# Layer 0's scan and attention as one stage, with the modulation products moved from VectorE to GpSimd and ScalarE

## The chip, the cores and the metric

The kernel runs on one core of a Trainium2 chip. The metric is the device time of one execution in microseconds (us); smaller is better. The core has five engines that run side by side and wait for each other through semaphores: PE (TensorE, matrix products), DVE (VectorE), ACT (ScalarE), POOL (GpSimd) and SP (SyncE, which here only issues transfers). Each engine takes its instructions strictly in the order in which the program has them.

## The reference, cut to what matters

A two-layer network works on 256 context tokens and 1024 latent tokens of width 1024. Layer 0's mixer has two independent halves that read the same projections, and it is these two that the change touches:

```
# half A: differential attention, 4 heads, 2 score maps per head, 128 queries a block in the reference
s = einsum('bhmqd,bhmkd->bhmqk', q, k) * 64**-0.5
p = softmax(s, axis=-1)
w = p[:, :, 0] - lam * p[:, :, 1]
o = einsum('bhqk,bhkd->bhqd', w, v)          # then an RMS norm per head

# half B: RWKV-7, 8 heads, a scan over the tokens, forward and backward
def step(S, inp):
    r_t, w_t, k_t, v_t, kk_t, a_t = inp
    sa = einsum('bhvk,bhk->bhv', S, kk_t)
    S = S * w_t - sa * (kk_t * a_t) + v_t * k_t
    return S, einsum('bhvk,bhk->bhv', S, r_t)
...
o = concatenate([attention, rwkv], axis=-1) @ w_out
```

Beside them stand the modulation vectors of the layer: `silu(c) @ mod_w + mod_b`, for the latent conditioning and for the context conditioning. Four of these vectors (g1, sh2, sc2, g2) are computed while the scan runs. Context queries (256) see only context keys, latent queries (1024) see all 1280.

## The kernel before

Everything is feature-major: a tile has 128 features on its partitions and tokens along its rows. Products that need precision use a split of fp32 into a high and a low part. The program is written as Python generators that yield between small pieces of work; a scheduler then orders each engine's instructions by its own estimate of when they can run, and semaphores are placed for that order. So the order on each engine is fixed before the run.

*Scan.* The 1280 tokens are cut into ten windows of 128 tokens, for both directions at once. A window has two chunks of 64 tokens, and each chunk is one `step`: four small groups of products on PE with an elementwise operation between each two (`rpm` on DVE, `sav` on ACT and DVE, the state `S` on DVE, the output copy `ryt` on ACT). What does not depend on the state is prepared ahead: `front` (scores L568, transposes L580, then `blocks`, a DVE chain that inverts 8 by 8 blocks) and `back` (`values` L609/L610, `inverse` L656, L662, L676, L687, which doubles the inverted blocks up to 64 and ends with the tile `iu`). In the loop `scan`, window sw runs beside `back` of window sw+1 and `front` of window sw+2: preparation stands up to two windows ahead. Before the first window, front 0, back 0 and front 1 run alone. `post` normalizes finished windows and stores them in `rw_o`.

*Modulation.* Every eighth round of the loop, `mods_dot` (L220) does two tiles: one DVE instruction multiplies a 128x1024 tile of transposed weights (`mdw`) with a row of the conditioning and sums it. That is 64 such instructions in this stage.

*Attention.* When the scan is through, `heads` runs over four heads and five pairs of query blocks. A score tile (L967, L968; 128 queries by up to 1280 keys, three PSUM banks) goes through a maximum on DVE (L970) and an exponential on ACT (L971). There are two such PSUM tiles, `at0` and `at1`. `differ` joins the two maps on DVE (L982); `mix` transposes the weights on PE (L999), copies them on ACT (`a_w`, L1001) and multiplies them with the values for 256 queries at once (`po`, L1004). `norm` then handles a whole head of 1280 tokens at a time and writes `at_o`.

PSUM has eight banks. In the scan five are `rw`, two `rz` and one `ry`; in the attention at0 and at1 have three each, and `mm` and `po` one each. After the attention comes the output projection (L87 to L89 with the tile `o`).

## Time and profile before

| what | us |
|---|---|
| median of 3 timed runs | 3969.39 (3968.36 to 3971.47) |
| the profiled execution: its own time | 3967.53 |
| its span, first to last instruction | 3965.7 |
| from the scan's first load (556.2) to the output projection's first product (1406.8) | 850.6 |
| of that, PE busy | 622.0 |
| mean granted clock of PE over the span | 0.935 |

A busy time is the union of an engine's instructions in a stretch, so the rest of the stretch is the time in which that engine stood idle. The granted clock is a share of 2.4 GHz; the engine has two levels, 1.2 and 2.4 GHz, so 0.79 means that part of the stretch ran at 0.5. PE's 622.0 us is the sum over the four stretches that the first group of rows shows.

### The profile page before, as it was taken

How to read it: one execution, taken by the hardware profiler on the slowest of the kernel's cores; microseconds unless marked ns; L12 is line 12 of the kernel's file. 1: busy time of each engine (PE TensorE's matmuls, PEld its weight loads, DVE VectorE, ACT ScalarE, POOL GpSimd, SP SyncE). 2: the span in 40 equal slices, each digit the busy share in tenths (PEclk: the TensorE clock that was granted, in tenths of full speed). 3: DMA queues.
4: the chain of work that ended last, by engine and by line, in shares of the span. 5: the costliest groups of instructions: out<-in, count | busy, mean ns of one | idle time of the engine just before them, and what ended most of it. 6: DMA issues, size and time to landing. Idle time of an engine off the chain costs nothing.

```text
span 3965.7 us, 68983 instructions
## 1 busy us (share of the span) xinstructions
PE 3587.8 (90%) x28912; PEld 2976.9 (75%) x28912; DVE 2048.2 (52%) x3741; ACT 1138.8 (29%) x1926; POOL 1305.6 (33%) x1121
## 2 busy tenths in 40 slices
PE   6999967766778879999999999999998889999998
PEld 4878846665667668888888888778776778888886
DVE  6344435766657647555444436357247663333335
ACT  3333321111255505111111113575543141111112
POOL 2455532322310015233222323217434352333223
PEclk8999977787788989999999999999999889999998
DMA  5244462333262142122222212232442311111111
GB/s 199 79 122 127 118 188 85 111 109 114 81 187 78 51 146 68 59 85 75 71 68 85 75 38 77 67 92 70 121 126 84 109 54 43 46 56 48 43 43 64
DMA packets 288999, 353.14 MB, mean 89 GB/s; under 512 B 91825, under 2 KB 217265, under 8 KB 288561
## 3 DMA queue, kind: packets, MB, share of 16 engines
q1 hardware_dynamic: 288688, 348.74, 28.3%
q8 instruction: 227, 3.72, 0.4%
q14 instruction: 84, 0.68, 0.1%
HBM read 265.03 MB, written 83.62 MB: 88 GB/s over the span
## 4 chain that ended last, share of the span: by engine, by line
PE 58%; DVE 3%; DMA 1%; ACT 1%; issue 1%; POOL 0%; SPq 0%; POOLq 0%; ACTq 0%; DVEq 0%
PE mm L87 10%; PE mm L88 10%; PE mm L89 10%; PE ss L87 4%; PE ss L88 4%; PE ss L89 4%; PE sp L88 4%; PE sp L87 4%; PE sp L89 4%; PE sp L1222 1%; PE ss L1475 1%; PE sp L1406 1%; PE si L1491 1%; PE mm L1232 1%; DMA wraw<-in_wout_dram 0%
## 5 line engine op out<-in xcount | busy, mean ns | idle before, releaser
L88 PE MATMUL mm<-actl,whi 128*128 128x512 f32 (+1 forms) x2432 | 903.3, 372 | 18.6 <-DVE actl L298 10.8
L87 PE MATMUL mm<-acth,whi 128*128 128x512 f32 (+1 forms) x2432 | 899.8, 372 | 19.2 <-ACT acth L95 6.9
L89 PE MATMUL mm<-acth,wlo 128*128 128x512 f32 (+1 forms) x2432 | 892.8, 370 | 0.0
L99 POOL TENSOR_TENSOR wlo<-wraw,whi 128x1024 fp32r<-128x1024 f32 (+2 forms) x243 | 495.7, 2047 | 1072.7 <-ACT whi L95 1065.4
L87 PEld LDWEIGHTS mm<-acth,whi 128*128 128x128 f32 x2432 | 465.1, 191 | 112.9 <-issue 8.1
L88 PEld LDWEIGHTS mm<-actl,whi 128*128 128x128 f32 x2432 | 465.3, 191 | 107.9 <-DVE actl L298 11.9
L89 PEld LDWEIGHTS mm<-acth,wlo 128*128 128x128 f32 x2432 | 465.0, 191 | 81.9 <-issue 4.4
L95 ACT CAST whi<-wraw 128x1024 fp32r<-128x1024 f32 (+2 forms) x243 | 217.1, 906 | 1049.5 <-PE mm L88 386.0
L345 POOL TENSOR_TENSOR relu<-relu 128x256 f32<-128x256 f32 (+1 forms) x163 | 162.2, 995 | 368.8 <-ACT relu L344 368.8
L97 DVE CAST hidh<-relu 128x256 fp32r<-128x256 f32 (+1 forms) x163 | 71.1, 436 | 354.8 <-POOL relu L345 353.6
L88 PE MATMUL sp<-hidl,whi 128*128 128x512 f32 (+1 forms) x648 | 238.5, 368 | 1.5 <-DVE hidl L99 1.5
L344 ACT ACTIVATE relu<-mm 128x256 f32<-128x256 f32 (+1 forms) x163 | 88.9, 545 | 520.8 <-PE mm L89 378.7
L87 PE MATMUL sp<-hidh,whi 128*128 128x512 f32 (+1 forms) x648 | 238.3, 368 | 0.0
L89 PE MATMUL sp<-hidh,wlo 128*128 128x512 f32 (+1 forms) x648 | 238.0, 368 | 0.0
L87 PE MATMUL ss<-hidh,whi 128*128 128x512 f32 (+1 forms) x600 | 222.8, 371 | 0.4 <-DVE hidh L97 0.4
L88 PE MATMUL ss<-hidl,whi 128*128 128x512 f32 (+1 forms) x600 | 222.5, 371 | 0.2 <-DVE hidl L99 0.2
L89 PE MATMUL ss<-hidh,wlo 128*128 128x512 f32 (+1 forms) x600 | 221.8, 370 | 0.0
L369 DVE SCALAR_TENSOR_TENSOR x<-ss,g,x 128x256 f32<-128x256 f32 x180 | 118.9, 661 | 145.2 <-PE ss L89 145.2
L369 DVE SCALAR_TENSOR_TENSOR x<-sp,g,x 128x512 f32<-128x512 f32 (+1 forms) x192 | 126.8, 661 | 105.5 <-PE sp L89 105.4
L220 DVE CUSTOM_DVE_ANT_0 mdj<-mdw,silu_r,t_cols 128x1024 f32<-128x1024 f32 x128 | 172.7, 1349 | 1.2
L369 DVE SCALAR_TENSOR_TENSOR x<-ss,g2b,x 128x512 f32<-128x512 f32 x120 | 90.0, 751 | 142.6 <-PE ss L89 142.6
L369 DVE SCALAR_TENSOR_TENSOR x<-sp,g2b,x 128x512 f32<-128x512 f32 (+1 forms) x132 | 96.7, 733 | 101.9 <-PE sp L89 101.9
(510 smaller groups left out, 6636.0 us busy)
## 6 DMA issues: line engine op xcount, KB each, us to landing
mdw<-in_modt_dram SPq DMA_DIRECT2D x80, 512.0 KB, 3.6
wraw<-in_wa_dram SPq DMA_DIRECT2D x64, 512.0 KB, 3.6
wraw<-in_wb_dram SPq DMA_DIRECT2D x64, 512.0 KB, 3.5
wraw<-in_win_dram SPq DMA_DIRECT2D x51, 512.0 KB, 3.8
x<-in_xT_dram SPq DMA_DIRECT2D x16, 640.0 KB, 10.7
rw_kr<-rw_t SPq DMA_DIRECT2D x16, 640.0 KB, 3.3
rw_bk<-rw_t SPq DMA_DIRECT2D x32, 320.0 KB, 3.9
rkr<-rw_kr SPq DMA_DIRECT2D x20, 512.0 KB, 5.1
```

What stands on the lines that cost most here:

```text
L87: self.nc.tensor.matmul(out, lh, rh, start=start and i == 0, stop=False)
L88: self.nc.tensor.matmul(out, lh, rl, start=False, stop=False)
L89: self.nc.tensor.matmul(out, ll, rh, start=False, stop=stop and i == n - 1)
L95: nc.scalar.copy(out=hi, in_=src)
L97: nc.vector.tensor_copy(out=hi, in_=src)
L99: e.tensor_tensor(out=lo, in0=src, in1=hi.bitcast(F32), op=ALU.subtract)
L220: nc.vector.tensor_tensor_reduce(out=junk, in0=raw, in1=rows[:, j], scale=1.0, scalar=modb[:, 8 * w + t : 8 * w + t + 1], op0=ALU.mult, op ...
L344: nc.scalar.activation(out=r, in_=ps, func=AF.Relu)
L345: nc.gpsimd.tensor_tensor(out=r, in0=r, in1=r, op=ALU.mult)
L369: nc.vector.scalar_tensor_tensor(out=xg, in0=ps, scalar=gate[:, m, j : j + 1], in1=xg, op0=ALU.mult, op1=ALU.add)
L1222: nc.tensor.matmul(pd, k["after" if d == 0 else "before"], rl.rearrange("p h t -> p (h t)"), start=d == 0, stop=d == 1)
L1232: nc.tensor.matmul(o, xd[d][:, hd * 64 : hd * 64 + 64], us[hd // 4, d][:, hd % 4], start=d == 0, stop=d == 1)
```

## The change

- *One stage.* `heads` is no longer run behind the scan but beside it: the loop `scan` takes a list of side tasks and advances the attention every third round and the modulation every fourth. Posts are advanced one at a time in each round (`output`).
- *One step ahead.* `front`, `values` and `inverse` of window sw+1 become one sequence, `prep`, that runs beside window sw. Buffers shrink accordingly (`rkr` 6 to 4, `rs` and `rbt` 10 to 6, `imb` 2 to 1 and others), and `rw` has three PSUM banks instead of five.
- *128 queries.* Attention goes block by block: `queries` loads one block of 128 in eight transfers (40 blocks instead of 20 pairs), there is one score tile `at` in PSUM instead of two, and `mix` multiplies 128 queries at a time. `norm` works in groups of up to 512 tokens.
- *Modulation.* `mods_mul` multiplies on POOL (L245 after the change) and sums on ACT (L246), in place of the single DVE instruction; each weight tile is loaded twice, once for each conditioning, so 64 loads instead of 32.

```
+    def mods_mul(self, pool, tag, bufs, modt, modb, which, names):
...
+            for j in range(2):
+                row = pool.tile([P, 1024], F32, name="silu_r", tag="silu_r", bufs=1)
...
+                for (t0, w), o in zip(which, outs):
+                    for t in range(8):
+                        raw = pool.tile([P, 1024], F32, name="mdw", tag="mdw", bufs=bufs)
+                        nc.sync.dma_start(out=raw, in_=modt[t0 + t])
+                        with self.tc.issue_after(self.last(E.Pool)), self.tc.issue_after(self.last(E.Activation)):
+                            nc.gpsimd.tensor_tensor(out=raw, in0=raw, in1=row, op=ALU.mult)
+                            nc.scalar.activation(out=raw, in_=raw, func=AF.Copy, accum_out=o[:, t, j : j + 1])
+                        yield
...
-        mb = T([P, 2, 2, 4, 64], "imb", 2)
-        kr = [T([P, 2, 4, P], "rkr", 6) for d in range(2)]
+        mb = T([P, 2, 2, 4, 64], "imb", 1)
+        kr = [T([P, 2, 4, P], "rkr", 4) for d in range(2)]
...
-                    s = T([P, 4, P], f"rs{hh}", 10)
+                    s = T([P, 4, P], f"rs{hh}", 6)
...
-                bt[d, c] = T([P, 4, P], "rbt", 10)
+                bt[d, c] = T([P, 4, P], "rbt", 6)
...
+    def prep(self, sw, o):
+        yield from self.front(sw, o)
+        yield from self.values(o)
+        yield from self.inverse(o)
+
+    def output(self):
+
+        while self.posts or self.written < 10:
+            if self.posts:
+                yield from self.posts.pop(0)
+            yield
+
+    def scan(self, pool, asides):
...
         for sw in range(10):
-            turn = [self.window(sw, os[sw])] + [self.back(os[sw + 1])] * (sw < 9) + [self.front(sw + 2, os[sw + 2])] * (sw < 8) + self.posts
-            self.posts = []
-            for q in count():
+            turn = [self.window(sw, os[sw])] + [self.prep(sw + 1, os[sw + 1])] * (sw < 9)
+            while turn:
                 turn = [g for g in turn if next(g, 0) is None]
-                if not turn:
-                    break
-                if q % 8 == 4:
-                    next(aside, None)
+                next(output, None)
+                q += 1
+                for every, steps in asides:
+                    if q % every == 0:
+                        next(steps, None)
+            os[sw].clear()
+        turn = [output] + [steps for _, steps in asides]
+        while turn:
+            turn = [g for g in turn if next(g, 0) is None]
...
+            for qb in range(10):
+                o = self.queries(hd, qb)
+                for m in range(2):
+                    self.scores(o, K, m)
+                    yield
+                    next(ahead, None)
+                    next(ahead, None)
+                    next(norm, None)
+                self.differ(o, qb)
                 yield from ahead
...
+        e = o["e"][m] = self.tile(f"a_e{m}", F32, bufs=3 - 2 * m)
+        ps = n.psum(1536, "at")
...
+            nc.tensor.matmul(ps[:, s], qh, K[m][:, s], start=True, stop=False)
+            nc.tensor.matmul(ps[:, s], ql, K[m][:, s], start=False, stop=True)
...
+        po = n.psum(512, "po")[:, :P]
...
+                for kb in range(k0 - 4, min(k0, nb)):
+                    nc.tensor.matmul(po, v[:, kb], ws[k0 // 4 - 1][:, kb % 4 * P : kb % 4 * P + P], start=kb == 0, stop=kb == nb - 1)
...
-        heads = L("at")
-        n.banks(("rw",), rw=5, rz=2, ry=1)
...
-        n.banks(("mm",), at0=1, at1=1, mm=1, po=1)
-        finish(at.heads(heads.__enter__(), rw.posts))
...
+        n.banks(("rw",), at=1, mm=1, po=1, rw=3)
+        with L("at") as ap, L("post") as rw.out, R("scan") as sp, n.pools(mo=1):
+            (g1, sh2, sc2, g2), mods = n.mods_mul(n.mo, "mm", 2, I["modt0"], k0["mod_b"], [(8 * q, 2 + q) for q in range(4)], ("g1", "sh2", "sc2", "g2"))
+            heads = at.heads(ap)
+            rw.scan(sp, ((3, heads), (4, mods)))
```

The order on the engines changes with it. First PE's row where the scan starts. Before, behind the last products of the projections stand the silu rows (L197) and then at once the scan's first scores (L568) and transposes (L580):

```order
L891 MATMUL sp<-ones,lam_pr 128x1 x2
L197 MATMUL rz<-ident,silu_c 128x128 x16
L568 MATMUL rw<-rkr,rbk 128x128 x8
L580 MATMUL rw<-ident,rbk 128x128 x4
L568 MATMUL rw<-rkr,rbk 128x128 x8
L580 MATMUL rw<-ident,rbk 128x128 x4
```

In the changed program score tiles of the first head (L1000, L1001) stand ahead of and between these same products, which are now L594 and L606:

```order
L1000 MATMUL at<-ak_4845,aq0h 128x256
L1001 MATMUL at<-ak_4845,aq0l 128x256
L1028 MATMUL mm<-ident,a_e_5111 128x128 x2
L1033 MATMUL po<-a_w,av 128x128 x2
L594 MATMUL rw<-rkr,rbk 128x128 x8
L606 MATMUL rw<-ident,rbk 128x128 x4
L1000 MATMUL at<-ak_4848,aq1h 128x512
L1001 MATMUL at<-ak_4848,aq1l 128x512
```

Fifteen score tiles (four of 256 keys, eleven of 1280) now come ahead of the first window's first product. The second place is PE's row in the middle of the scan, between two of the products that double an inverse. Before, pieces of other windows of the scan stand there (scores, a step's first and second product):

```order
L568 MATMUL rw<-rkr,rbk 128x128 x8
L709 MATMUL rw<-S,rkr 64x64 x16
L662 MATMUL rw<-id,iwt 32x32 x64
L580 MATMUL rw<-ident,rbk 128x128 x4
L715 MATMUL rw<-rpm,iu 64x64 x16
```

In the changed program the same product (L662 is now L684) stands between pieces of attention alone, here in window 3:

```order
L678 MATMUL rw<-itt,rs_8158 32x32
L1033 MATMUL po<-a_w,av 128x128 x2
L1000 MATMUL at<-ak_7335,aq0h 128x512
L1001 MATMUL at<-ak_7335,aq0l 128x512
L1000 MATMUL at<-ak_7335,aq0h 128x512
L1001 MATMUL at<-ak_7335,aq0l 128x512
L1000 MATMUL at<-ak_7335,aq0h 128x256
L1001 MATMUL at<-ak_7335,aq0l 128x256
L684 MATMUL rw<-id,iwt 32x32 x64
L1028 MATMUL mm<-ident,a_e_8919 128x128 x4
```

So a score tile and its mixing took the place of other windows' scan work. Counted over the windows 0 to 9, 0, 4, 6, 9, 4, 7, 4, 5, 6 and 2 tiles of 1280 keys stand between the first product of a window and that of the next; six more stand behind the last window. The third place is POOL's row in window 0. Before, the masked copies `imb` follow one another:

```order
L575 TENSOR_TENSOR imb<-rs_4777,t_masks_85 64x256
L575 TENSOR_TENSOR imb<-rs_4780,t_masks_85 64x256
L575 TENSOR_TENSOR imb<-rs_4800,t_masks_85 64x256
L575 TENSOR_TENSOR imb<-rs_4803,t_masks_85 64x256
L575 TENSOR_TENSOR imb<-rs_4823,t_masks_85 64x256
```

In the changed program (L575 is now L601) products of the modulation stand between them:

```order
L601 TENSOR_TENSOR imb<-rs_4839,t_masks_85 64x256
L601 TENSOR_TENSOR imb<-rs_4842,t_masks_85 64x256
L245 TENSOR_TENSOR mdw<-mdw,silu_r 128x1024 x2
L601 TENSOR_TENSOR imb<-rs_4964,t_masks_85 64x256
L601 TENSOR_TENSOR imb<-rs_4967,t_masks_85 64x256
L245 TENSOR_TENSOR mdw<-mdw,silu_r 128x1024
L601 TENSOR_TENSOR imb<-rs_5032,t_masks_85 64x256
L601 TENSOR_TENSOR imb<-rs_5035,t_masks_85 64x256
L245 TENSOR_TENSOR mdw<-mdw,silu_r 128x1024
```

So a masked copy that the inversion waits for can now stand behind a product of 128x1024.

## Rows read from the trace of the kernel before

**Rows 1.** Busy time by engine in five stretches: scan start, windows 0-8, window 9, attention, projection.
```profile
core 0: us, PE busy (x) PEld busy (x) DVE busy (x) ACT busy (x) POOL busy (x), PEclk, DMA share, GB/s
556.20:613.90 57.70, 34.62 (x865) 30.06 (x865) 22.59 (x54) 7.63 (x13) 14.35 (x22) 0.62 0.41 121
613.90:1071.40 457.50, 319.42 (x10015) 286.73 (x10015) 311.69 (x699) 84.43 (x152) 123.20 (x142) 0.79 0.34 106
1071.40:1099.00 27.60, 17.59 (x342) 14.59 (x340) 10.66 (x36) 6.68 (x14) 10.07 (x8) 0.88 0.35 96
1099.00:1406.80 307.80, 250.34 (x1301) 201.06 (x1301) 193.60 (x306) 159.56 (x282) 32.29 (x55) 0.89 0.34 102
```

**Rows 2.** PE groups of the scan: busy, mean ns | idle before, releasers.
```profile
L715 PE MATMUL rw<-rpm,iu 64*64 64x64 f32 x576 | 28.8, 272 | 49.0 <-DVE rpm L712 49.0
L656 PE MATMUL rw<-itt,rs 32*32 32x32 f32 x2560 | 32.7, 204 | 32.5 <-DVE itt L652 19.2 <-issue 13.1
L709 PE MATMUL rw<-S,rkr 64*64 64x64 f32 x576 | 29.4, 271 | 25.2 <-DVE S L729 15.0 <-DVE ipr L631 5.9 <-issue 4.3
```

**Rows 3.** Timeline (start, duration) of window 0's preparation, which runs alone.
```profile
556.17 0.33 SPq L557 DMA_DIRECT2D rkr<-rw_kr  x1
561.47 2.08 PE L568 MATMUL rw<-rkr,rbk 64*128 64x128 f32 x16 [10.60 <-DMA rbk<-rw_bk]
573.64 0.73 POOL L575 TENSOR_TENSOR imb<-rs,t_masks 64x256 f32<-64x256 f32 x1
584.82 0.71 DVE L652 STREAM_TRANSPOSE itt<-id 128x512 f32<-128x512 f32 x1 [1.20 <-POOL id L636]
591.22 0.71 DVE L652 STREAM_TRANSPOSE itt<-id 128x512 f32<-128x512 f32 x1
607.61 0.69 DVE L692 COPY iu<-rw 32x512 f32<-32x512 f32 x1 [2.21 <-ACT iu L694]
```

**Rows 4.** Timeline of PE in the attention: one score tile, transposes, a mix, a norm.
```profile
1123.94 0.50 PE L967 MATMUL at<-ak,aqh 128*128 128x512 f32 x1
...
1125.08 0.28 PE L968 MATMUL at<-ak,aql 128*128 128x256 f32 x1
1342.08 0.60 PE L999 MATMUL mm<-ident,a_e 128*128 128x128 f32 x4
1342.51 1.03 PE L1004 MATMUL po<-a_w,av 128*128 128x256 f32 x4
1346.07 1.16 PE L1031 MATMUL mm<-ident,rsy_at 128*128 128x128 f32 x8
```

**Rows 5.** Groups of DVE and ACT that a score tile goes through.
```profile
L970 DVE TENSOR_REDUCE a_mx<-at 128x1 f32<-128x1280 f32 x64 | 94.6, 1486 | 21.8 <-PE at L968 21.4
L971 ACT ACTIVATE a_e<-at,a_mx 128x1280 f32<-128x1280 f32 x64 | 85.2, 1331 | 44.4 <-DVE a_mx L970 29.9 <-PE mm L999 12.6 <-DVE rsa_at L120 0.8
L971 ACT ACTIVATION_READ_ACCUMULATOR a_e<-at,a_mx 128x1 f32 x80 | 15.8, 198 | 0.0
L982 DVE SCALAR_TENSOR_TENSOR a_e<-a_e,a_f,a_e 128x1280 f32<-128x1280 f32 x32 | 50.5, 1580 | 1.2
```

**Rows 6.** Groups: the modulation on DVE in this stage, and POOL's products of 1024 columns.
```profile
L220 DVE CUSTOM_DVE_ANT_0 mdj<-mdw,silu_r,t_cols 128x1024 f32<-128x1024 f32 x64 | 88.2, 1379 | 0.8
L99 POOL TENSOR_TENSOR wlo<-wraw,whi 128x1024 fp32r<-128x1024 f32 x179 | 430.5, 2414 | 920.8 <-ACT whi L95 915.0 <-PE mm L89 5.8
```

**Rows 7.** Timeline of the attention: a DVE instruction alone, and beside a long POOL instruction.
```profile
1220.80 0.22 DVE L980 SCALAR_TENSOR_TENSOR a_f<-a_r,lam_n,a_z 128x1 f32<-128x1 f32 x1
1227.29 2.90 POOL L99 TENSOR_TENSOR a_ol<-a_o,a_oh 128x1280 fp32r<-128x1280 f32 x1 [6.28 <-DVE a_r L977]
1228.52 1.69 DVE L980 SCALAR_TENSOR_TENSOR a_f<-a_r,lam_n,a_z 128x1 f32<-128x1 f32 x1
```

**Rows 8.** One head's query loads on SP: duration of one issue, min/median/max ns.
```profile
L951 SPq DMA_DIRECT2D aqh<-at_q1h x20: 445/566/597, 1154.3 to 1199.1; - x20
```

**Rows 9.** Timeline of the end of the attention.
```profile
1381.50 0.37 ACT L1006 COPY a_o<-po 128x256 f32<-128x256 f32 x1 [1.22 <-PE po L1004]
1383.27 2.53 PE L1019 MATMUL mm<-ones,a_oh 128*128 128x1 f32 x20 [1.81 <-ACT a_oh L1014]
1393.58 2.08 PE L1031 MATMUL mm<-ident,rsy_at 128*128 128x128 f32 x8 [0.84 <-DVE a_o L1033]
1406.79 0.55 PE L87 MATMUL mm<-o,whi 128*128 128x256 f32 x1 [11.13 <-DMA o<-rw_o]
```

More of the change, by code (lines that the diff above doesn't have):

```diff
@@ L223, in steps @@
                         yield
+        return outs, steps()
+    def mods_mul(self, pool, tag, bufs, modt, modb, which, names):
+        nc, E = self.nc, mybir.EngineType
+        outs = [self.const.tile([P, 8, 2], F32, name=nm) for nm in names]
+        def steps():
+            for j in range(2):
+                row = pool.tile([P, 1024], F32, name="silu_r", tag="silu_r", bufs=1)
+                for half in range(2):
+                    ps = self.psum(512, tag)
+                    for q in range(4):
+                        nc.tensor.matmul(ps[:, q * P : q * P + P], self.silu_c[:, half * 4 + q, j : j + 1].to_broadcast([P, P]), self.ident,
+                                         start=True, stop=True)
+                    nc.scalar.copy(out=row[:, half * 512 : half * 512 + 512], in_=ps)
+                for (t0, w), o in zip(which, outs):
[6 more added lines that the diff above has]
+                        yield
+            for (t0, w), o in zip(which, outs):
+                nc.gpsimd.tensor_tensor(out=o, in0=o, in1=modb[:, 8 * w : 8 * w + 8].unsqueeze(2).to_broadcast([P, 8, 2]), op=ALU.add)
         return outs, steps()
@@ L744, in step @@
                 if w in self.half:
-                    self.posts.append(self.post(self.out, w, d, y, "rz" if sw < 9 else "mm"))
+                    self.written += 1
+                    self.posts.append(self.post(self.out, w, d, y, "mm"))
                 else:
@@ L1006, in mix @@
-        nc.scalar.copy(out=oT[:, qp * 256 : qp * 256 + 256], in_=po)
-        if qp == 4:
-            self.whole = oT, rz
+                for kk in range(w):
+                    nc.tensor.transpose(ps[:, kk * P : kk * P + P], e[:, (k0 + kk) * P : (k0 + kk) * P + P], n.ident)
+                ws.append(tl("a_w", F32, 512, 2))
+                nc.scalar.copy(out=ws[-1][:, : w * P], in_=ps[:, : w * P])
+            if k0:
+                for kb in range(k0 - 4, min(k0, nb)):
+                    nc.tensor.matmul(po, v[:, kb], ws[k0 // 4 - 1][:, kb % 4 * P : kb % 4 * P + P], start=kb == 0, stop=kb == nb - 1)
@@ L1010, in norm @@
+            if k0 < nb:
+                yield
+        nc.scalar.copy(out=oT[:, qb * P : qb * P + P], in_=po)
     def norm(self, hd, oT, rz):
         n, nc, tl = self.n, self.nc, self.tile
-        sq = tl("a_oh", F32)
-        nc.scalar.activation(out=sq, in_=oT, func=AF.Square)
-        yield
-        yield
-        ss = n.psum(10, "mm")
-        for b in range(10):
-            nc.tensor.matmul(ss[:, b : b + 1], sq[:, b * P : b * P + P], n.ones, start=True, stop=True)
+        ss = n.psum(512, "mm")[:, :10]
@@ L1020, in norm @@
+        for g0, gn in ALL_GROUPS:
+            sq = tl("a_oh", F32, 512, 2)
+            nc.scalar.activation(out=sq[:, :gn], in_=oT[:, g0 : g0 + gn], func=AF.Square)
+            for b in range(gn // P):
+                c = g0 // P + b
+                nc.tensor.matmul(ss[:, c : c + 1], sq[:, b * P : b * P + P], n.ones, start=True, stop=True)
         ms = self.pool.tile([P, 10], F32, name="a_ms", tag="a_ms", bufs=1)
```

176 lines of the change are left out of this document (65 added, 111 removed).

## The prediction

> **What bounds the kernel now.** The change touches only what lies between the scan's first load at 556.2 us and the output projection's first product at 1406.8: 850.6 us of the span. I read the windows view first, because one busy share over both stages would hide that they have different limits [rows 1]. The scan start takes 57.7 us. The nine windows 0 to 8 take 457.5 us, 50.8 each, of which PE works 319.42 / 9 = 35.5 and stands for 15.3; its granted clock there is 0.79, so part of it ran on the lower of the two levels, 1.2 instead of 2.4 GHz. Window 9, which has no preparation beside it, takes 27.6 us, and attention up to the projection 307.8 at a clock of 0.89. PE is busy for 622.0 of the 850.6 us and idle for 228.6. That is the room that running both halves together could use, and PE's work is the floor under any such gain.
>
> Next the groups, to see what PE waits for in the scan [rows 2]: for `rpm` from DVE (49.0 us before L715), for `itt` from DVE (19.2 of 32.5 before L656), for the state `S` (15.0 of 25.2 before L709). These are hops of short chains, not a shortage of any engine: DVE is busy for 311.69 of the 457.5 us, and 88.2 of that are the modulation's products [rows 6], which no chain waits for.
>
> Then the timeline of window 0's preparation, the only one that runs alone [rows 3]. It goes from the load of `rkr` at 556.17 to the last `iu` at 607.61 + 0.69 = 608.30. The first score stands at 561.47, so the chain takes 47 us: 13 for the front up to the last `imb` (573.64 + 0.73), then about 34 for blocks and inverse. Two `itt` 6.4 us apart are one stage of two half-steps, so a half-step takes 3.2 us.
>
> Last what a score tile goes through. On PE its products run from 1123.94 to 1125.36 [rows 4]; I take 1.25 us of work. Then comes the maximum with 1.49, the exponential with 1.33 and its sum with 0.20 [rows 5]. Nothing else can be written to that tile meanwhile: a cycle of about 4.5 us with a hop. Before, two tiles alternate; after, there is one.
>
> **The change part by part.**
>
> *Start of the scan.* The scan's loads now stand on SP behind query loads that wait for small score tiles, some 4.5 us; the chain then starts at 566 and ends, alone, 47 later. Eleven big tiles stand on PE between its products. Each of the six half-steps of the inverse (3.2 us) then stands behind a tile whose cycle is 4.5: about 2 more each, 12 in all. 566 + 47 + 12 = 625, which is 69 us. Bounds: 57.7 (all tiles fit into waits), and 4 x 1.8 + 11 x 4.5 + 47 = 104 (end to end; a small tile has a fifth of the keys, but the same hops and fixed costs; I take 1.8).
>
> *One step ahead.* Preparation of window sw+1 now has to begin and end beside window sw, where it had two windows before. The state steps take 27.6 us (window 9) [rows 1]. If front and steps overlapped fully, blocks and inverse would still follow; I take 27.6 + 34 less 5, since the last step's products need not be through before the next chain runs: 57 us a window without attention. Bounds: 50.8 (as now) and 61.7 (no overlap). Nine windows: 513, bounds 457 and 555.
>
> *Attention beside it.* A tile's own PE work is 1.25 for scores, 0.7 for half of ten blocks of transposes (0.60 for four), and 1.2 for half of a mix, 3.1 us together [rows 4]. The window of 57 us has 57 - 35.5 = 21.5 us of idle PE; five tiles a window (45 stand in the nine) want 15.5. On paper all fits. But the order is fixed, and each piece of attention that stands before a late chain product delays it, as each late maximum holds up PE. I take half of the work as hidden, 1.55 a tile, between bounds of 0 and 3.1: 45 x 1.55 = 70.
>
> *128 queries a block.* The mix has twice as many products of half the width: eight of 128 columns took 1.16 us where four of 256 took 1.03 [rows 4], so PE's time is about the same for the same work. The query loads go from 160 to 320 issues at 566 ns [rows 8], 91 us more on SP spread over some 700; SP's cover is that attention has a whole window for four or five blocks. If that cover is gone, the cost falls on a tile's cycle, not on the scan.
>
> *Modulation.* DVE loses 64 x 1379 ns = 88.2 us [rows 6]. ACT gains 64 sums of 1024 columns; an exponential of 1280 with its read is 1.53, so at most 98 us. POOL gains 64 products of 128x1024: no such fp32 product with a fp32 result stands in the trace; the nearest, with a rounded result, takes 2414 ns [rows 6], so up to 154 us. Both have room: Over the four stretches POOL goes to about 14 + 123 + 10 + 32 + 154 = 333 of some 730 us, ACT to 8 + 84 + 7 + 160 + 98 = 357 [rows 1]. I cost it at nothing, since the engines are idle for half the stage; what it costs without that cover is the GpSimd rival below. A gain from the freed DVE I also put at nothing: these instructions stand mostly in its waits. The other 32 loads of 512 KB are on DMA engines with a third of their time used [rows 1].
>
> *Window 9 and the tail.* Window 9 with two tiles: 27.6 + 2 = 30. Then six tiles are left, without other work, at a full cycle: 27. Behind them the last group is normed. Before, from the last copy of `a_o` at 1381.50 to the last product of the norm at 1395.7 are 14 us, and 11.13 more to the projection, which waited for a load of `o` [rows 9]. I take 14 + 5 for the norm, its DVE work and store, and 5 for the load of pieces: 24. Tail 51.
>
> *Sum.* 69 + 513 + 70 + 30 + 51 = 733 against 850.6: 117.6 us less. The profiled execution took 3967.53; less 117.6 this is 3849.9. The median of the runs is 1.9 above that execution, so the forecast is 3852.
>
> **The rivals.**
>
> *Attention's own PE work lies on the path* (3.1 a tile). For it: PE's clock of 0.79, so that more work need not fit into the same time; against it: the 21.5 us of idle PE. 45 x 1.55 = 70 more: 803, time 3922.
>
> *Attention is wholly hidden* (0 a tile). For it: the sum of idle PE, and denser work may raise the clock, as 0.88 and 0.89 outside the windows show [rows 1]. 663, time 3782.
>
> *The single tile runs the scan* (slower). PE takes instructions in order. If each score tile waits for its predecessor's exponential, and the scan's product behind it too, then a tile costs the scan a whole cycle: 4.5 x 45 = 202 in place of 70. 865, time 3984. It decides for slower from (850.6 - 663) / 45 = 4.2 us a tile. For it: the products of the inverse have only attention between them now. Against it: a chain that is waiting for DVE loses nothing by PE's wait beside it.
>
> *GpSimd's products hold up DVE.* In the attention a DVE instruction of one column takes 0.22 us alone and 1.69 beside a POOL instruction of 2.90, and both end at about 1230.2 [rows 7]: it was held until POOL was through. 64 new products stand among the masks of the inversion and beside DVE's chains. Where one starts first, a DVE instruction waits on average half of 2.41 us, less when DVE was idle; I take 1.0: 64 more, 797, time 3916. The Trainium skill (SBUF — State Buffer, "Who interferes with whom") says that a DVE instruction with two SBUF inputs contends with a GpSimd instruction that reads SBUF, and that whichever comes second is blocked entirely until the other is through. The trace's 1.69 against 0.22 agrees. By that rule, with every product blocking a chain for all its 2.41 us, the sum would be 733 + 154 = 887, and the change slower by 36; I hold that for an extreme, since PE waits for DVE in only part of each window.
>
> *No change*: the gains and the single tile cancel, near 3969.
>
> **How the numbers follow.** Chances: forecast 0.48 (own range 3800 to 3910), attention on the path 0.17, wholly hidden 0.13, the single tile 0.12, GpSimd 0.07, no change 0.03. With the low bounds together, 69 + 457 + 0 + 30 + 51 = 607, the time would be 3726; with the high ones, 69 + 555 + 140 + 30 + 51 = 845, it would be 3964. For 8 in 10 I leave out the slower cases and the lower half of the hidden one: 3775 to 3945. A difference of 0.2%, 8 us, is about what a measurement of this kernel can tell from none. Faster by more: 0.84; within: 0.04; slower: 0.12.
>
> **What would show it.** In the profile after: window 0's first step product near 625; windows 65 us apart on average, longest where nine tiles stand (window 3), shortest with two to four; PE's clock above 0.79 in the windows. Before score tiles PE should wait for the exponential of the previous tile; where these waits exceed 1.5 us a tile and end last, the single tile is at work. POOL's new products should take 2.4 us or less, and DVE's short instructions should not lengthen beside them; if they do, it is the GpSimd rival. From the last step product to the first projection product I expect about 50 us, and that product near 556.2 + 733 = 1289. The forecast is wrong if windows stay at 57 or less (hidden) or reach 78 (single tile), or if a wait that I did not price ends last: SP's query loads, or the loads of the projection behind them.

## The result and the profile after

The change made the kernel slower. The median of five runs is 3993.85 us (3988.06 to 4010.78) against 3969.39 before; the ratio is 1.0070, 95% interval 1.0044 to 1.0096. The forecast was 3852, with 3775 to 3945 as its range. The profiled execution took 3988.7 us, 21.2 more than the one of before. Of all runs told of below, a few executions ran at a far lower granted clock throughout (0.43 to 0.75 over the span instead of about 0.93), and the medians leave them out.

The windows view of the changed kernel, over scan start, windows 0 to 8, and window 9 up to the output projection (start:end, length, busy time of each engine with its number of instructions, granted clock, DMA share), answers to [rows 1]:

```profile
core 0: us, PE busy (x) PEld busy (x) DVE busy (x) ACT busy (x) POOL busy (x), PEclk, DMA share, GB/s
556.20:633.50 77.30, 50.74 (x859) 41.87 (x858) 42.74 (x76) 24.73 (x45) 11.18 (x22) 0.76 0.42 121
633.50:1338.30 704.80, 567.99 (x11303) 489.10 (x11301) 388.77 (x811) 265.68 (x511) 289.70 (x254) 0.82 0.40 118
1338.30:1430.50 92.20, 73.70 (x701) 62.70 (x700) 46.64 (x82) 39.12 (x78) 29.02 (x24) 0.80 0.50 172
...
sum 874.30, PE 692.42 PEld 593.67 DVE 478.15 ACT 329.52 POOL 329.90; mean PE 230.81 PEld 197.89 DVE 159.38 ACT 109.84 POOL 109.97
```

The stage takes 874.3 us where 733 were forecast and 850.6 were before. A window takes 704.8 / 9 = 78.3 us instead of 65. PE stands for 704.8 - 568.0 = 136.8 us in the nine windows, as much as before (457.5 - 319.4 = 138.1), though 45 score tiles now lie beside the scan: attention did not fill the idle time of PE. Nor did the clock rise much: 0.82 after 0.79.

The waits view for the same windows shows what stands behind that (who waited <- for whom: us in all, times, longest). First ACT and POOL:

```profile
ACT mdw L246 <- POOL mdw L245: 128.2, 46, 8.6
...
POOL mdw L245 <- DMA mdw<-in_modt_dram: 88.8, 22, 10.1
```

Then, in the same view, DVE, which waits for ACT's copies and POOL's masks, PE, and SP (this one over the whole stage):

```profile
DVE sav L738 <- ACT sav L737: 29.8, 16, 6.2
DVE imc L642 <- POOL imb L601: 29.1, 8, 7.3
...
PE rw L678 <- DVE itt L674: 23.2, 10, 9.6
PE at L1000 <- ACT a_e L1004: 19.2, 9, 4.9
PE mm L824 <- POOL po_y L821: 18.1, 6, 7.6
PE rw L594 <- ACT ryt L758: 11.6, 3, 4.8
PE po L1033 <- ACT a_w L1030: 8.0, 6, 3.5
PE mm L1028 <- ACT a_w L1030: 7.8, 6, 4.9
...
PE rw L630 <- ACT ryt L758: 5.5, 1, 5.5
...
SPq L243 <- ACT mdw L246: 179.5, 44, 25.9
```

The largest of the waits shown are at the instructions of the modulation that the forecast had costed at nothing: ACT stood 128.2 us with a sum at its head (L246) that had no product yet, POOL 88.8 us with a product (L245) whose weights had not come, SP 179.5 us with a load whose buffer the last sum had not left. PE's wait for the exponential of the one score tile, which the forecast's slower rival was built on, is only 19.2, 0.4 us a tile. A long wait of ACT, POOL or SP is no loss by itself, since these engines have idle time to spend: POOL waits longest for operands of the masks (`imb`, 101.2 us), and without any modulation it waits longer for them (170.4). What counts is what PE and DVE wait for behind such an instruction.

The timeline of the changed kernel shows one such chain from end to end, early in window 1:

```profile
714.58 2.36 POOL L245 TENSOR_TENSOR mdw<-mdw,silu_r 128x1024 f32<-128x1024 f32 x1
715.74 1.16 PE L594 MATMUL rw<-rkr,rbk 64*128 64x128 f32 x16
716.97 1.06 ACT L246 ACTIVATE mdw<-mdw 128x1024 f32<-128x1024 f32 x1 [2.50 <-POOL mdw L245]
717.40 1.27 DVE L599 TENSOR_TENSOR rs<-rw,t_masks 128x512 f32<-128x512 f32 x2
718.14 0.33 SPq L243 DMA_DIRECT2D mdw<-in_modt_dram  x1
722.18 2.34 POOL L245 TENSOR_TENSOR mdw<-mdw,silu_r 128x1024 f32<-128x1024 f32 x1 [5.25 <-DMA mdw<-in_modt_dram]
724.48 1.52 POOL L601 TENSOR_TENSOR imb<-rs,t_masks 64x256 f32<-64x256 f32 x2
724.55 1.06 ACT L246 ACTIVATE mdw<-mdw 128x1024 f32<-128x1024 f32 x1 [6.44 <-POOL mdw L245]
725.61 0.56 ACT L758 COPY ryt<-rw 128x512 f32<-128x512 f32 x1
726.03 1.99 DVE L642 TENSOR_REDUCE imc<-imb 128x128 f32<-128x1024 f32 x1 [7.35 <-POOL imb L601]
726.23 0.37 PE L630 MATMUL rw<-sav,rs 64*64 64x64 f32 x1 [5.50 <-ACT ryt L758]
```

A weight tile's load starts at 718.14, once the sum ahead (716.97) has left the buffer. The next product is already at POOL's head and waits for it until 722.18. The two masks `imb` behind it had their operand from DVE at 717.40 + 1.27 = 718.67, and run at 724.48. DVE stands 7.35 us before the inversion (`imc`); the masks' own 1.52 would have been needed in any case, so 5.8 us of that are the wait behind the product. On ACT the next sum waits for that product, and behind it the copy `ryt`, which empties one of the three `rw` banks; PE needs that bank at 726.23 and has stood 5.50. So in this stretch one late load holds up four engines that had work at hand.

The product itself takes what was assumed (a row of the page, against [rows 6]):

```profile
L245 POOL TENSOR_TENSOR mdw<-mdw,silu_r 128x1024 f32<-128x1024 f32 x64 | 157.5, 2464 | 96.4 <-DMA mdw<-in_modt_dram 88.8
```

And the tail (against [rows 9]): the scan's last product ends at 1363.2, 24.9 us after the start of window 9 where 30 were forecast, and the projection's first product starts 67.3 us later where about 50 were expected. The last norm product stands at 1427.63 and the first output product at 1430.55, with no wait for `o` between them, which the forecast had allowed 5 us for.

```profile
1362.07 1.15 PE L755 MATMUL rw<-rs,sav 128*64 128x64 f32 x32
...
1427.63 2.08 PE L1058 MATMUL mm<-ident,rsy_at 128*128 128x128 f32 x8 [0.79 <-DVE po_y L841]
1430.55 0.58 PE L87 MATMUL mm<-o,whi 128*128 128x256 f32 x1 [0.84 <-DVE a_o L1060]
```

### The profile page after: what moved, and what is told of

Same layout as the page of the kernel before. It is cut to its first block, busy times and chain, and to the rows that moved or that the text cites. A ratio compares the mean times of both kernels' runs of the same rounds, so it can differ in the third digit from the quotient of the medians.

```text
span 3986.9 us, 70179 instructions
## 1 busy us (share of the span) xinstructions
PE 3653.2 (92%) x29248; PEld 3036.8 (76%) x29248; DVE 1985.4 (50%) x3621; ACT 1208.8 (30%) x2102; POOL 1458.8 (37%) x1197
## 4 chain that ended last, share of the span: by engine, by line
PE 58%; DVE 4%; ACT 1%; DMA 1%; issue 0%; POOL 0%; POOLq 0%; SPq 0%; ACTq 0%; DVEq 0%
PE mm L87 10%; PE mm L88 10%; PE mm L89 10%; PE ss L87 4%; PE sp L87 4%; PE sp L88 4%; PE ss L88 4%; PE sp L89 4%; PE ss L89 4%; PE sp L1249 1%; PE ss L1502 1%; PE sp L1433 1%; PE si L1518 1%; PE mm L1259 0%; PE sp L1207 0%
## 5 line engine op out<-in xcount | busy, mean ns | idle before, releaser
L245 POOL TENSOR_TENSOR mdw<-mdw,silu_r 128x1024 f32<-128x1024 f32 x64 | 157.5, 2464 | 96.4 <-DMA mdw<-in_modt_dram 88.8
```

Source lines behind the costliest of these rows:

```text
L245: nc.gpsimd.tensor_tensor(out=raw, in0=raw, in1=row, op=ALU.mult)
```

## The experiments

Times are medians; the changed kernel's 3993.85 and before's 3969.39 are the two to hold them against, and ratios are to before in the same runs. The scheduler orders each kernel anew, so every edit also moves other instructions. Below, two edits that only take products away make a kernel 15 and 29 us slower; so a difference of some 20 us need not come from what the edit was meant to change, and only the larger ones are clear of that. The theory after the result: instructions of the modulation that wait at the head of ACT's and POOL's queues hold the scan behind them (the queue theory). Its rivals: contention of GpSimd with DVE; the longer chain of preparing one step ahead; PE's own work; the one score tile.

**Attention apart.**

```
-            rw.scan(sp, ((3, heads), (4, mods)))
+            rw.scan(sp, ((4, mods),))
+            finish(heads)
```

> The changed kernel, but attention runs behind the scan again (still by 128 queries, one score tile, one step ahead, modulation on GpSimd). If the forecast's term for preparation one step ahead is right, a window without attention takes 57 us; if the longer chain of one step ahead is what failed, it takes 68 or more, near the 78 us measured with attention beside it. The attention alone, 64 big tiles at one cycle of 4.5 us, takes about 300 us. So about 4030 us in all with 57 us windows, 4130 with 68.

Measured: 4198.14, ratio 1.0586 (1.0557 to 1.0614), more than either total expected. Two rows of its windows view, windows 0 to 8 and the attention:

```profile
623.60:1202.30 578.70, 387.27 (x10162) 336.18 (x10160) 244.23 (x607) 154.28 (x286) 261.87 (x217) 0.67 0.37 113
1235.00:1643.10 408.10, 278.11 (x1585) 237.66 (x1585) 183.14 (x283) 161.02 (x315) 34.11 (x58) 0.82 0.23 71
```

The windows without attention take 64.3 us each, between the two expectations, and the attention behind them 408 us, where 300 were expected and 307.8 is the time of before. So the changed form of the attention (one tile, blocks of 128 and what goes with them) costs some 100 us when nothing lies beside it, and the forecast's cycle of 4.5 us a tile was too short.

**No modulation.** The calls of `mods` are dropped and the four outputs are set to zero.

> The changed kernel without the modulation of this stage (no loads, no products, no sums; four vectors are set to zero instead). If GpSimd's products hold up DVE and POOL's own short work for the scan, the windows fall from 78 us by 5 or more each, 50 to 70 us in all. If PE's own work and its order set the windows, less than 15 us.

Measured: 3898.86, ratio 0.983 (0.9805 to 0.9856): 95 us faster than the changed kernel, more than the 50 to 70 expected. One row of its windows view and some of its waits view, all for windows 0 to 8:

```profile
630.80:1252.00 621.20, 534.16 (x11269) 461.61 (x11268) 371.47 (x808) 201.73 (x389) 138.40 (x189) 0.87 0.29 83
```

```profile
DVE sav L738 <- ACT sav L737: 11.7, 14, 1.4
...
DVE imc L642 <- POOL imb L601: 5.8, 7, 1.0
...
PE rw L678 <- DVE itt L674: 27.2, 9, 9.2
PE at L1000 <- ACT a_e L1004: 16.7, 12, 3.6
PE mm L824 <- POOL po_y L821: 9.3, 6, 2.3
...
PE mm L1028 <- ACT a_w L1030: 1.4, 3, 0.7
...
PE po L1033 <- ACT a_w L1030: 1.2, 5, 0.5
```

A window takes 69.0 us. The reader can see how a wait counts twice here. PE's idle time falls from 136.8 to 621.2 - 534.2 = 87.0 us, 50 less; and PE's busy time falls by 34 for nearly the same instructions, most of it with the clock, which is granted at 0.87 instead of 0.82 (a share of (1 - 0.87) x 2 = 0.26 of 621 us at 1.2 GHz, 161 us, instead of 254). 50 + 34 = 84 us in the windows; about 7 more lie in scan start and tail, the rest behind the stage and in the spread of the runs.

Set against the PE rows of the changed kernel above, these rows say where the 50 us of idle time were. PE's waits for ACT's copies `ryt` and `a_w`, which share ACT's queue with the sums, fall from 32.9 to 2.6 us, and those for POOL's `po_y`, which shares POOL's queue with the products, from 18.1 to 9.3. Its wait for the inversion (`itt`), on whose chain the masks lie, does not fall (23.2 to 27.2), although DVE's wait for the masks does (29.1 to 5.8). DVE's busy time falls by 17 us (388.77 to 371.47) for three instructions fewer: that is what contention with GpSimd can have added to DVE's own instructions in the changed kernel.

**Modulation on DVE.**

```
-                            nc.gpsimd.tensor_tensor(out=raw, in0=raw, in1=row, op=ALU.mult)
-                            nc.scalar.activation(out=raw, in_=raw, func=AF.Copy, accum_out=...)
+                            nc.vector.tensor_tensor_reduce(out=raw, in0=raw, in1=row, ..., accum_out=...)
```

> The changed kernel with the modulation's product and sum as one DVE instruction again (64 of about 1.38 us, in place; still 64 loads). If the products on GpSimd are the loss, 30 to 60 us faster than the changed kernel; if DVE's room is what the merged stage needs, up to 88 us slower; if PE sets the time, within 10 us of it.

Measured: 3963.62, ratio 0.9985 (0.9969 to 1.0002): 30 us faster than the changed kernel, with 86 us more work on DVE (its 64 instructions of the modulation). ACT's and POOL's waits for the modulation are gone, but each load still comes only once the buffer is free. 65 us of the modulation's 95 are left, although none of it stands in ACT's or POOL's queue any more.

**Alternating score products.** `tc_after` puts each product behind the PE instruction written just before it.

```
+                        with self.tc_after(i + hh > 0):
                             nc.tensor.matmul(ps[hh][...], bk[d][rows, i, c], kr[d][rows, :, i, tok], ...)
```

> The changed kernel, with an order edge that keeps the scan's score products alternating between the upper and the lower 64 rows of PE, as they were before the change. In the changed kernel half of these 40 groups run as 8 products of one half and then 8 of the other, at 112 ns each instead of 36 and 76 in turn: about 0.9 us more for each of 20 groups. If PE's work is on the path this wins 15 to 18 us; if the wait for the second bank of three takes its place, nothing or a loss.

Measured: 3975.01, ratio 1.0019 (1.0004 to 1.0034): 19 us faster than the changed kernel, as expected. Two rows of the changed kernel's timeline, both at a granted clock of 1.00, show what such an order costs: 8 products of one half take as long as 16 that alternate (the row at 715.74 above).

```profile
584.73 1.16 PE L594 MATMUL rw<-rkr,rbk 64*128 64x128 f32 x8
```

PE's groups of these products, in the changed kernel up to the end of window 8 and in this run (where they are L595), show 15 of the 19 us:

```profile
L594 PE MATMUL rw<-rkr,rbk 64*128 64x128 f32 x640 | 80.7, 318 | 19.1 <-ACT ryt L758 11.6 <-issue 5.8 <-DVE iu L713 1.0
L595 PE MATMUL rw<-rkr,rbk 64*128 64x128 f32 x640 | 65.4, 320 | 16.2 <-ACT ryt L762 7.8 <-issue 5.6 <-ACT rbt L609 1.3
```

**No attention beside, no modulation.** The two edits of the first two runs together.

> Attention behind the scan and no modulation in the stage (four vectors set to zero instead). It shows the price of preparing one step ahead by itself. The forecast had 57 us a window. If the 64.3 us of the run with attention apart come from the modulation's place on GpSimd and ScalarE, the windows fall to 55 to 59 us; if they come from the longer chain of one step ahead or from three PSUM banks, they stay above 62.

Measured: 4145.04 (one run, so every figure that rests on it rests on a single execution). From the windows view of this run, windows 0 to 8 and the attention:

```profile
620.60:1142.30 521.70, 364.77 (x10148) 318.81 (x10146) 237.50 (x606) 90.60 (x166) 122.52 (x154) 0.68 0.22 67
1175.00:1578.10 403.10, 273.59 (x1584) 234.62 (x1584) 184.41 (x283) 159.56 (x313) 32.67 (x58) 0.83 0.23 70
```

521.7 / 9 = 58.0 us a window: the forecast's 57, with three banks in that price. That the number fits is partly luck: the clock in these windows is 0.68, where the forecast's rows had 0.79 and its term for one step ahead says nothing of the clock. The scan's score products show a side result:

```profile
L594 PE MATMUL rw<-rkr,rbk 64*128 64x128 f32 x640 | 57.3, 323 | 11.5 <-DMA rbk<-rw_bk 10.6 <-DMA sav<-rw_vt 0.9
```

With three banks, but nothing beside the scan, they take 57.3 us, less than the 80.7 of the changed kernel and at a lower clock. So the smaller number of banks alone did not spoil their order.

**Modulation spread over three steps.**

```
+                        nc.sync.dma_start(out=raws[q], in_=modt[work[q][0]])
...
+                            nc.gpsimd.tensor_tensor(out=raws[q - 1], in0=raws[q - 1], in1=row, op=ALU.mult)
...
+                            nc.scalar.activation(out=raws[q - 2], in_=raws[q - 2], func=AF.Copy, accum_out=...)
```

> The changed kernel with the same products and sums, but three weight tiles in place of two, the load issued a step before the product and the sum a step behind it, so that neither GpSimd nor ScalarE should find its operand missing. If the loss is work that queues behind a waiting modulation instruction (ScalarE stood 128 us before the sums, GpSimd 89 us before the products), 50 to 80 us faster than the changed kernel, near the 3899 us without modulation. If the loss is contention between GpSimd's products and DVE, less than 20 us faster.

Measured: 3967.43, ratio 1.0005 (0.9988 to 1.0022): 26 us faster than the changed kernel, half of what the queue theory expected and a little more than the rival's 20. The edit took the waits away only in part: POOL still waits 63.7 us for weights (88.8 before the edit) and ACT 67.2 for products (128.2). So it does not decide between the two.

**Mix for 256 queries.**

```
-                ahead = self.mix(qb, v, o)
+                ahead = self.mix(qb // 2, v, first, o)
```

> The changed kernel with the mix for 256 queries at once, as before the change (transposes of two blocks together, products of 256 columns; scores, buffers and single score tile as in the changed kernel, one more buffer of weights). PE's mix took 96.5 us busy where it took 75.4 before. If PE's own work is on the path, 10 to 20 us faster than the changed kernel; if chains and waits set the windows, within 8 us of it.

Measured: 4007.57, ratio 1.0104 (1.0089 to 1.0119): 14 us slower than the changed kernel, outside both branches. The mix's products took 103.6 us instead of 109.6. With so little saved, the run does not show what PE's own work costs; it shows only that going back to 256 queries does not win the loss back.

**Both: alternating and on DVE.**

> Alternating score products and the modulation on DVE together. If the two losses are independent, their gains add: 19 + 30 us under the changed kernel, about 3945, and so faster than both kernels. If they share a wait, between 3950 and 3965.

Measured: 3967.31, ratio 0.9998 (0.9985 to 1.0010). That is no faster than the modulation on DVE alone (3963.62). The gains did not add; the miss shows that 19 us from one order need not hold in another.

**Parts of the modulation.** Three runs, each leaving out one part:

```
-                            nc.scalar.activation(out=raw, in_=raw, func=AF.Copy, accum_out=...)
```

> The changed kernel with the modulation's loads and GpSimd's products, but without ScalarE's sums of them (the four vectors are set to zero instead). Without any modulation the changed kernel took 3899 us, with all of it 3994. If the loss is ScalarE's queue, which stands behind each sum until the product is there, this run comes to 3900 to 3925. If it is GpSimd's queue (masks of the inversion behind a product that waits for its weights) or contention, it stays above 3960.

```
-                            nc.gpsimd.tensor_tensor(out=raw, in0=raw, in1=row, op=ALU.mult)
```

> The changed kernel with the loads and ScalarE's sums, but without GpSimd's products (the vectors are then sums of raw weights). If GpSimd's products and what queues behind them are the loss, 3900 to 3930. If it is ScalarE's sums themselves and their wait, which now is for the weights' load, it stays above 3950.

```
-                        nc.sync.dma_start(out=raw, in_=modt[t0 + t])
-                            nc.gpsimd.tensor_tensor(out=raw, in0=raw, in1=row, op=ALU.mult)
+                            nc.gpsimd.tensor_tensor(out=raw, in0=same, in1=row, op=ALU.mult)
```

> The changed kernel with all products and sums, but of one weight tile that is loaded once (63 loads of 512 KB left out). If the waits start with weights that come late (GpSimd stood 89 us for them), 40 to 70 us faster than the changed kernel. If the order alone makes the queues wait, less than 20 us.

Measured, with ratios to before: 3974.39 without sums (1.0011, 1.0000 to 1.0022; 19 us of the 95), 3944.06 without products (0.9937, 0.9916 to 0.9958; 50), 3971.61 without loads (1.0002, 0.9990 to 1.0015; 22). The first came out on the branch of GpSimd's queue or contention, the other two between their branches. No single part is the loss; the products are the largest, and without them loads and sums still cost 45 us. DVE's wait for the masks is 29.1 us with all, 27.4 without sums, 8.4 without products, 9.6 without loads: a product that finds its weights there hardly holds the masks; one that waits for them does. But the run without loads, which took that wait away, won only 22 us.

Part of the reason stands in DVE's busy time in windows 0 to 8 (third busy figure), here without sums and without loads:

```profile
633.00:1320.00 687.00, 554.25 (x11313) 478.87 (x11312) 408.21 (x814) 206.53 (x398) 288.73 (x253) 0.83 0.41 122
634.90:1311.40 676.50, 549.60 (x11312) 472.95 (x11310) 402.85 (x814) 268.89 (x518) 289.28 (x256) 0.86 0.26 77
```

For six instructions more than without any modulation (371.47) DVE is busy 37 and 31 us longer (a few us of it are these six), where the changed kernel has 17. So with part of the waits gone, DVE's instructions beside GpSimd lengthened more, and what these two runs won is net of that.

**Masks on DVE.**

```
-                    nc.gpsimd.tensor_tensor(out=mb[rows, d, c], in0=s[rows, :, 0:64], ...)
+                    nc.vector.tensor_tensor(out=mb[rows, d, c], in0=s[rows, :, 0:64], ...)
```

> The changed kernel with the inversion's masked copies (80 products of 64x256) on DVE instead of GpSimd, so that none of them stands behind a modulation product; the modulation stays on GpSimd and ScalarE. DVE gets some 25 to 40 us more work. If the queue on GpSimd is the larger part of the products' loss, 10 to 30 us faster than the changed kernel in spite of that; if contention with DVE is, as slow as the changed kernel or slower.

Measured: 3983.34, ratio 1.0031 (1.0015 to 1.0047): 10 us faster than the changed kernel with 52 us more work on DVE in the windows. This leans to the queue, but by no more than the spread of the changed kernel's own runs.

**Less PE work.** The products with the low part of the queries are left out.

```
-            nc.tensor.matmul(ps[:, s], ql, K[m][:, s], start=False, stop=True)
```

> The changed kernel without the low part of the attention's scores (half of the score products left out; PE is busy with them for 50.5 us of the stage). If PE's own work is on the path, 40 to 60 us faster than the changed kernel. If the tile's cycle through DVE and ScalarE and the chains of the scan set the windows, less than 20 us.

Measured: 4023.30, ratio 1.0130 (1.0113 to 1.0147): 29 us slower with less work. ACT's wait for products rose from 128.2 to 171.3 us, and DVE's for ACT's `sav` from 29.8 to 53.2. The order of the instructions is another one, and these waits grew with it. So the same edit without the modulation:

> The changed kernel without the modulation and without the low part of the scores. Without the modulation alone it took 3899 us. If a tile's price in the windows is PE's own work, the 50 us of products left out give 25 to 50 us: 3850 to 3875. If it is the tile's cycle through DVE and ScalarE, less than 15 us.

Measured: 3914.39, ratio 0.9867 (0.9851 to 0.9884), 15 us more than without the modulation alone. Its windows view:

```profile
634.80:1268.80 634.00, 524.41 (x11122) 451.26 (x11121) 371.18 (x808) 202.00 (x389) 138.70 (x189) 0.82 0.28 81
```

Beside the row without modulation: 147 products fewer, PE idle for 109.6 us instead of 87.0, and the clock at 0.82 instead of 0.87; busy time fell by only 10. Neither branch holds. Fewer products did not shorten a window, and what lengthened it is PE's waits; but since busy time hardly fell, what PE's own work would cost at an unchanged clock is not shown.

**The modulation before the change.** In the kernel before, `rw.scan(sp, mods)` gets an empty list and the outputs are set to zero.

> The kernel before without the modulation of this stage (the 64 DVE products and 32 loads left out, four vectors set to zero). The forecast took these instructions to stand mostly in DVE's waits, and so a gain from freeing DVE at nothing. If that holds, less than 15 us faster than before; if they were on the chain, 30 to 88 us.

Measured: 3929.36, ratio 0.9903 (0.9888 to 0.9918): 39 us faster than before. Missed: those 64 DVE instructions did not lie in waits. Its row for windows 0 to 8:

```profile
617.10:1032.00 414.90, 305.12 (x10015) 273.21 (x10014) 228.92 (x569) 85.01 (x153) 107.81 (x140) 0.83 0.24 75
```

A window falls from 50.8 to 46.1 us.

**Towards a faster version.** Modulation on DVE with attention every second round (`(2, heads)` for `(3, heads)`), then with the weights loaded a step ahead into three tiles, then with alternating score products as well:

```
-            rw.scan(sp, ((3, heads), (4, mods)))
+            rw.scan(sp, ((2, heads), (4, mods)))
...
+                        nc.sync.dma_start(out=raws[q], in_=modt[work[q][0]])
...
+                            nc.vector.tensor_tensor_reduce(out=raws[q - 1], in0=raws[q - 1], in1=row, ..., accum_out=...)
...
+                        with self.tc_after(i + hh > 0):
```

> The modulation on DVE as in that run (3964 us), and attention advanced every second round instead of every third. If a tile costs the windows the same wherever it stands (about 2.2 us) and a full cycle of 4.5 behind the last window, the six tiles of the tail win 10 to 15 us: about 3950. If denser tiles run into the one score tile, the windows lengthen by as much or more: 3965 to 3990.

> Modulation on DVE with its weights loaded a step ahead (three tiles), attention every second round. DVE waited 19 us for weights in the windows of the run without the early load; if those were on the path, 3935 to 3945; if they were hidden, 3955 as without it.

> The same with the scan's score products kept alternating. In the changed kernel that won 19 us, beside the modulation on DVE nothing. If PE's work counts once the weights come early, 3925 to 3940; if not, as the run without it.

Measured: 3954.94, ratio 0.9952 (0.9936 to 0.9969); 3954.66, 0.9952 (0.9935 to 0.9969); and 3942.20, 0.9927 (0.9912 to 0.9943). The last is faster than both kernels, by 27 us than before and by 52 than the changed one. The early load by itself won nothing, and alternating products on top of it 12, where 15 to 30 or nothing was expected. The windows view of the last run:

```profile
646.10:1328.80 682.70, 564.18 (x11500) 484.65 (x11498) 455.22 (x952) 220.46 (x423) 156.49 (x197) 0.84 0.39 118
1328.80:1380.40 51.60, 27.31 (x403) 22.45 (x402) 20.73 (x50) 8.60 (x19) 14.39 (x11) 0.60 0.77 267
```

The windows take 75.9 us with all attention in them but its end, and the tail falls from 92.2 to 51.6.

## Why the prediction was wrong

**The step that failed** is the modulation: "I cost it at nothing, since the engines are idle for half the stage". Measured, it costs the changed kernel 95 us (3993.85 against 3898.86). The shares of busy time on which that rested came out as foreseen: POOL 330 us (333 forecast), ACT 330 (357). What they leave out is order. A product and a sum wait at the head of their queues, 88.8 and 128.2 us, and what stands behind them is needed by the scan and the attention: masks, `po_y`, `sav`, `ryt`, `a_w`. PE's waits for `ryt`, `a_w` and `po_y` are 39 us longer than without the modulation, most of its 50 us of added idle time, and the lower granted clock (0.82 against 0.87) goes with most of the other 34. The prediction named the waiting queue as something to look for on SP and for score tiles. Its GpSimd rival saw the products among the masks and priced their contention, but not what a product holds up that itself waits for a load.

How the 95 us divide between waiting queues, contention and the work itself stays open. The runs that took one part away won 19 to 50 us; contention with DVE is 17 us of DVE's busy time in the changed kernel and 31 and 37 in the two runs where parts of the waits are gone; and on DVE, in no queue of ACT or POOL, the modulation would still cost 65.

**A gain from the freed DVE at nothing** was the second error in the same term: the modulation cost 39 us before. The prediction read from [rows 6] that no chain waits for these products, and no row it showed could tell. The change moved work that cost 39 us to where it costs 95; on DVE in the merged stage it costs 65 (3963.62 against 3898.86).

The sum, term by term (forecast, then measured; rows two to four each compare runs of different order and clock):

| term | forecast | measured |
|---|---|---|
| scan start | 69 | 77.3 |
| nine windows, one step ahead, nothing beside | 513 | 522 (58.0 each) |
| attention beside them | 70 | 99 (69.0 - 58.0 each) |
| modulation in the windows | 0 | 84 (78.3 - 69.0 each) |
| window 9 and tail | 81 | 92.2 |
| stage | 733 | 874.3 |

One step ahead came out within its error, but at a clock that the forecast had not foreseen. Against before without the modulation, a window is 58.0 - 46.1 = 11.9 us longer, and of the 107 us in nine windows 364.77 - 305.12 = 60 are PE busy for longer with nearly as many products, at 0.68 instead of 0.83; the other 47 are idle time. Attention beside the scan was about half hidden, as the mechanism said, only larger: from the run with neither beside the scan to the one with attention alone, PE's busy time grows by 169 us (with the clock rising from 0.68 to 0.87), its idle time takes up 70 of that, and 99 come on top, 2.2 us a tile for 1.55. The mix in blocks of 128, put at about the same PE time, took 109.6 us busy instead of 88.1; going back to 256 did not make the kernel faster. The last term hides two errors that partly cancel: window 9 took 24.9 us for 30, the tail 67.3 for 51. Whether a tile delays the scan by its work on DVE and ACT, by the order on PE, by PE's own work or by the lost pairs stays open.

**The rivals.** The single tile gave 865 us for the stage and windows of 78, near the 874 and 78.3 measured, but by chance: the same tile with no modulation beside it runs at 69.0 us a window, with PE waiting 16.7 us for it (19.2 in the changed kernel). Nor are windows longest where most tiles stand: window 3 with nine takes 81.8 us, window 6 with four 87.3. GpSimd holding up DVE was right in kind: DVE's instructions lengthened by 17 us in all, in keeping with [rows 7], where the rival had 64. Beside that stands what it did not have, DVE and PE waiting for POOL's other work in order behind a product that itself waited for a load. The rule of the Trainium skill that was weighed there (SBUF — State Buffer, "Who interferes with whom") is not contradicted by that: 17 us of DVE's busy time are its size in the changed kernel, and that 887 us, its extreme, lies near the result is chance.

**Where the gain of the merge went.** Both without modulation, the changed kernel takes 3898.86 us and the one with attention apart 4145.04: running the halves together is worth 246 us (the second figure is a single run). Against before without modulation (3929.36) 30 of them are left. One step ahead takes (58.0 - 46.1) x 9 = 107, attention by itself 403 us instead of 307.8, 95 more; 13 are not attributed. So 202 of the 246 us go into the forms that the merge was given, one step ahead and one score tile with blocks of 128; which of their parts costs what, and how much of it is the clock, was not tested. The modulation, 95 instead of 39, turns the 30 into a loss of 24.

## What to carry to other kernels

An engine that is busy for a third of the time is not free: ask of every instruction put on it what it waits for, and what stands behind it in that engine's order. Work that depends on a load of its own, with two buffers, is best put where nothing that another engine waits for is queued behind it; no place that was tried here does that: on DVE it still cost 65 us, and a third buffer on GpSimd and ScalarE won 26 of the 95. And price what a moved piece costs in the old place by a run without it before calling it hidden.

## What the runs showed of the hardware

Products of 64 rows on the upper and the lower half of PE run at the same time if they alternate: 16 in 1.16 us, and 8 of one half alone also 1.16, both at a granted clock of 1.00. In the changed kernel about half of the 40 groups lost that. The Trainium skill (TensorE: Matmul & The Clock Gate, "Part 3: Packing small matmuls — row/col tiling") says that products in distinct row groups run concurrently; the trace agrees, and adds that the order of the products decides whether they do.

A run with fewer products can come out longer, at a lower clock: 147 products fewer in the windows, PE idle for 109.6 us instead of 87.0, granted clock 0.82 instead of 0.87, and 13 us longer. The order of the instructions differs too, so the missing products alone are not shown to be the cause. The Trainium skill (TensorE: Matmul & The Clock Gate, "What's actually happening") has the throttled state as the default that activity releases; these two rows agree.

The same GpSimd products lengthened DVE's work by different amounts: DVE's busy time in the windows is 371.47 us without the modulation, 388.77 with it, and 408.21 with its products but without the sums (three to six instructions more than the first).
